# Feature-major products with the tokens' high and low halves side by side in one 512-column matmul

## The chip, the core and the metric

The kernel runs on one core of a Trainium2 chip. The metric is the device time of one execution in microseconds (us); lower is better. TensorE is called PE here, VectorE DVE, ScalarE ACT, GpSimd POOL, and SyncE (which issues the weight transfers) SP. PEld is TensorE's loading of the stationary operand.

## The reference

The program computes two transformer blocks on 256 tokens of width 1024, in float32. The first block (latent attention beside a gated convolution, then a 32-expert mixture) is not touched by the change. The second block is, cut to what matters:

```python
u = rms_norm_2(h, norm_mix)
proj = u @ w_in                       # z_pool 512, q 512, k 128, v 128, g_pool 1024, g_attn 1024
y_pool = multiscale_pool(z_pool, w_pool_group, pool_scale) @ w_pool_branch
y_attn = windowed_gqa(q, k, v, sink) @ w_attn_branch
merged = sigmoid(g_pool) * y_pool + sigmoid(g_attn) * y_attn
h = h + merged @ w_out
u = rms_norm_2(h, norm_ffn)
h = h + (silu(u @ w_ffn_gate) * (u @ w_ffn_up)) @ w_ffn_down   # hidden width 2816
return rms_norm_2(h, norm_final)
```

## The kernel before

A matrix product is made of three products of rounded halves: a float32 value is split into a high half (a rounded copy, made by ACT) and a low half (the rest, a subtraction on DVE), and `high*high + high*low + low*high` is accumulated in one PSUM tile. `mm3` (L275) issues these three matmuls for each piece of 128 contracted rows.

The weights come as one stream of pieces of 128x1024 values (two to one DMA of 1 MB, tile `raw`, seven buffers). `Stream.split` casts a piece to its high half `whi` on ACT (L116) and subtracts to get the low half `wlo` on DVE (L119), each in a ring of five buffers; `W.ahead` keeps up to four pieces split ahead of the one in use, and `W.take` hands out the next. A cast of a new piece waits until PE has finished with the piece five before it, whose buffer it takes.

In block 2 a product is either "rows" (tokens stationary, 512 columns of weights moving) or "feature-major" (weights stationary, the 256 tokens moving, output 128 features x 256 tokens). The feature-major ones are made by `features` (L287): eight pieces k, each with three matmuls of 256 columns: weights' high half with the tokens' high half (L279), weights' high half again with the tokens' low half (L280), weights' low half with the tokens' high half (L281). The transposed tokens are in `uTh` and `uTl` (attention and pooling) and `u2h` and `u2l` (feed-forward), each 128 x 8 x 256. One piece of weights (128x1024) is just what one feature-major product uses.

The feature-major products through `u_block` and `ff_first` are, in order: four of the pooling input (`zp`, `pool_in`, L1362), eight gates of the pooling branch (`gt` into `gp`, L1396), eight gates of the attention branch (`gt` into `ga`), and in the feed-forward part, for each of 20 hidden blocks f, a gate and an up product (`gu`, `ff_first`, L1553). In between stand the small products of the attention: scores (`s2a`, `s2b`), transposed probabilities (`pT`), values (`av`), and the pooling groups' products (`pg`, L1387), and later the branch products (`br`) and the output product (`o`). The result in PSUM is multiplied on DVE by `R`, the tokens' norm factors spread over all partitions (L1367, L1399, L1559), and then pooled, or sent through Tanh or Silu on ACT.

In the feed-forward loop (L1597) each f issues the down product (`f`, "rows") of block f-2 (nine matmuls of 512 columns and six of 256), then gate and up of f; after the loop stand the down products of blocks 18 to 21. `hidden` splits the activated block into `sh` (ACT) and `sl` (DVE).

PSUM tiles come from two pools of four (`mmt`, `acct`). A scheduler puts each engine's instructions in order from the order in which the code issues them, its own costs, and the data they need; the queues then run strictly in that order.

Of the kernel before, what the change touches and what calls it, by code (L numbers as in the profile page):

```python
# [11 lines left out]
F32 = mybir.dt.float32  # L12
F32R = mybir.dt.float32r
BF16 = mybir.dt.bfloat16
I32 = mybir.dt.int32
AF = mybir.ActivationFunctionType
ALU = mybir.AluOpType
# [3 lines left out]
P = 128  # L21
D = 1024
NM = 16
S = 256
# [34 lines left out]
def block_kernel(ctx, tc, rwt, x, meta, pos, wst, gains, cst, pvec, rbias, sink, wpg, cst2, out):  # L59
    nc = tc.nc  # L60
    PE, ACT, DVE, POOL = nc.tensor, nc.scalar, nc.vector, nc.gpsimd
# [5 lines left out]
    def mmt(name):  # L67
        return ps.tile([P, 512], F32, name=name, tag="mm", bufs=4)
# [110 lines left out]
    W = Stream()  # L179
# [20 lines left out]
    def sm(w, p=P):  # L200
        return keep.tile([P, w], F32, name=f"sm{w}", tag=f"sm{w}", bufs=12)[:p]
# [49 lines left out]
    def stt(o, a, sc, b, op0=ALU.mult, op1=ALU.mult):  # L251
        return DVE.scalar_tensor_tensor(o, a, sc, b, op0=op0, op1=op1)  # L252
# [15 lines left out]
    small, pace, last_mm = [], [1], [None]  # L268

    def fill(n=None):  # L270

        for _ in range(len(small) if n is None else min(n, len(small))):
            small.pop(0)()

    def mm3(o, pairs, first=True, last=True):  # L275

        n = len(pairs)
        for i, (sh, sl, mh, ml) in enumerate(pairs):
            PE.matmul(o, sh, mh, start=first and i == 0, stop=False, skip_group_check=True)  # L279
            PE.matmul(o, sh, ml, start=False, stop=False, skip_group_check=True)  # L280
            last_mm[0] = PE.matmul(o, sl, mh, start=False, stop=last and i == n - 1, skip_group_check=True)  # L281
            fill(pace[0])

    def kb(w, k, n=P):
        return w[:, k * n:(k + 1) * n]

    def features(o, w, ah, al, c0, n):  # L287

        mm3(o, [(kb(w[0], k), kb(w[1], k), ah[:, k, c0:c0 + n], al[:, k, c0:c0 + n])
                for k in range(8)])  # L290

    def rows(o, w, ah, al, n, first, last):

        mm3(o, [(ah, al, kb(w[0], n, 512), kb(w[1], n, 512))], first=first, last=last)
# [82 lines left out]
    with tc.tile_pool(name="p1", bufs=1) as p1:  # L377
# [3 lines left out]
        start = ExitStack()  # L381
# [69 lines left out]
        def in_block(name, c0, n, psum=mmt):  # L451
            o = psum(name)[:, :n]
            features(o, W.take(), hth, htl, c0, n)
            return o
# [21 lines left out]
        o, w = mmt("cq")[:, :S], W.take()  # L476
        for z, (wz, az) in enumerate(((0, hth), (0, htl), (1, hth))):
            for k in range(8):
                PE.matmul(o, kb(w[wz], k), az[:, k, NM:], start=z + k == 0, stop=z == 2 and k == 7,
                          skip_group_check=True)  # L480
# [55 lines left out]
        R = p1.tile([P, T], F32, name="R")  # L536
# [118 lines left out]
        w = W.take()  # L655
        for j in range(4):
            o = mmt("kn")[:, :T]
# [208 lines left out]
    with tc.tile_pool(name="p2", bufs=1) as p2:  # L866
# [3 lines left out]
        th = p2.tile([P, 2, D], F32R, name="tkh")  # L870
        tl = p2.tile([P, 2, D], F32R, name="tkl")
# [11 lines left out]
        o = mmt("lg")  # L883
        for i in range(2):
            for k in range(8):
                PE.matmul(o[:, i * 36:(i + 1) * 36], tT[:, k, i * P:(i + 1) * P], kb(rw, k, 36), start=k == 0,
                          stop=k == 7, skip_group_check=True)
# [55 lines left out]
        for c in (0, S):  # L943
            for i in range(2):
                oh_ins = DVE.tensor_scalar(oh[:, i, c:c + S], cs[:, C_IOTA + c:C_IOTA + c + S], code[:, i:i + 1],
                                           None, op0=ALU.is_equal)
        PE.matmul(rk[:, 8:16], ones, gz[:, 1:].rearrange("p a b -> p (a b)"), start=True, stop=True,
                  skip_group_check=True)
# [158 lines left out]
        for ex in range(N_EXP):  # L1107
            g, e = divmod(ex, 8)
            xg = xgs[g][:, :D], xgs[g][:, D:]
            gu = mmt("gu")  # L1110
# [56 lines left out]
        with tc.If(many > 0):  # L1167
# [11 lines left out]
            for g in range(4):  # L1179
# [3 lines left out]
                for b in range(2):  # L1183
                    for a in range(4):
                        for i in range(2):
                            for src in (th, tl):
                                PE.matmul(kb(pa, a), kb(src[:, i], 4 * b + a).bitcast(F32), ohx[:, i],
                                          start=i == 0 and src is th, stop=i == 1 and src is tl,
                                          skip_group_check=True)
# [44 lines left out]


    with tc.tile_pool(name="p3", bufs=1) as p3:
        uTh = p3.tile([P, 8, S], F32R, name="uTh", tag="th")
        uTl = p3.tile([P, 8, S], F32R, name="uTl", tag="tl")
        with tc.tile_pool(name="p3a", bufs=1) as q3:
            c2 = q3.tile([P, 64 + 512], F32, name="c2")  # L1240
            POOL.dma_start(c2, cst2)
# [8 lines left out]
            R = q3.tile([P, S], F32, name="R2")  # L1250
# [3 lines left out]
            def pw(name):  # L1254
                return q3.tile([P, PW], F32, name=name, tag="pw", bufs=5)

            def u_block(name):
                o = mmt(name)[:, :S]
                features(o, W.take(), uTh, uTl, 0, S)
                return o  # L1260


# [99 lines left out]
            def pool_in(g):  # L1362
                zp = pw("zp")
                POOL.memset(zp[:, :8], 0.0)
                POOL.memset(zp[:, 8 + S:], 0.0)
                o = u_block("zp")
                DVE.tensor_mul(zp[:, 8:8 + S], o, R)  # L1367
                W.ahead()
                s, lo, hi = zp, 0, PW
                for m in range(g + 1):  # L1370
                    d = pw("ws")
                    a, b = (1, 0) if m == 0 else (2 ** (m - 1), 2 ** (m - 1))
                    lo, hi = lo + a, hi - b
                    DVE.tensor_add(d[:, lo:hi], s[:, lo - a:hi - a], s[:, lo + b:hi + b])
                    s = d
                w = 2.0 ** (g + 1)
                res = pw("res")[:, :S]
                stt(res, s[:, 8:8 + S], 1.0 / w, zp[:, 8:8 + S], ALU.mult, ALU.subtract)
                for c0 in (0, S - 8):
                    e = c2[:, g * 16:g * 16 + 8] if c0 == 0 else c2[:, g * 16 + 8:g * 16 + 16]  # L1380
                    DVE.tensor_mul(res[:, c0:c0 + 8], s[:, 8 + c0:16 + c0], e)
                    DVE.tensor_sub(res[:, c0:c0 + 8], res[:, c0:c0 + 8], zp[:, 8 + c0:16 + c0])
                return res
# [12 lines left out]
            def gates(dst, js):  # L1396
                for j in js:
                    o = u_block("gt")
                    DVE.tensor_mul(dst[:, j], o, R)  # L1399
                    ACT.activation(dst[:, j], dst[:, j], AF.Tanh, scale=0.5)  # L1400
                    W.ahead()

# [36 lines left out]
            def branch(gt, sh, sl, js, done=None):  # L1439
                for j in js:  # L1440
# [8 lines left out]
                    if done:  # L1449
                        done(j)  # L1450

            res = [pool_in(0)]
            scores2(0, 0)
            scores2(0, 2)
            es0 = softmax2(0)
            pool_group(0, res[0])
            res.append(pool_in(1))
            scores2(1, 0)
            scores2(1, 2)
            es1 = softmax2(1)  # L1460
            pool_group(1, res[1])
            res.append(pool_in(2))
            denom(0, es0)
            pTx = [q3.tile([P, 2, 512], F32, name="pTa", **kw) for kw in ({}, {"tag": "q4"})]
# [4 lines left out]
            pool_group(2, res[2])  # L1469
            values2(0, 0)  # L1470
            gates(gp, (0, 1))
            pool_group(3, res[3])
            values2(0, 1)
            denom(1, es1)
            probs_T2(1, 0)
            at0 = attn_out(0)
            gates(gp, (2, 3))
            probs_T2(1, 1)
            values2(1, 0)
            gates(gp, (4,))  # L1480
            values2(1, 1)
            at1 = attn_out(1)
# [27 lines left out]
            nx = [normed(0, o2[0], g_f2, s2)]  # L1510
            with tc.issue_after(merged[0].ins):
                ACT.activation(sm(1), ones[:, :1], AF.Silu)
            u2h = p3.tile([P, 8, S], F32R, name="u2h", tag="th")
            u2l = p3.tile([P, 8, S], F32R, name="u2l", tag="tl")

            def first_T(k):
                if k == 5:
# [4 lines left out]
        with tc.tile_pool(name="p3b", bufs=1) as q3:  # L1522
            R = q3.tile([P, S], F32, name="R3")
            hids = {}

            def hidden(f, src, c0=0, n=S):
                if f not in hids:
                    hids[f] = (q3.tile([P, S], F32R, name="sh", tag="sh", bufs=6),
                               q3.tile([P, S], F32R, name="sl", tag="sl", bufs=6))
                split(src, *[t[:, c0:c0 + n] for t in hids[f]])  # L1530
# [20 lines left out]
                    hidden(f, kb(ht, f), i * P, P)  # L1551

            def ff_first(f):  # L1553
                o = mmt("gu2")
                for b in range(2):
                    features(o[:, b * S:(b + 1) * S], W.take(), u2h, u2l, 0, S)
                    W.ahead()
                gu = q3.tile([P, 2, S], F32, name="gu", tag="gu", bufs=2)
                DVE.tensor_tensor(gu, o.rearrange("p (a t) -> p a t", a=2),  # L1559
                                  R[:, None, :].to_broadcast([P, 2, S]), op=ALU.mult)  # L1560
                ACT.activation(gu[:, 0], gu[:, 0], AF.Silu)
                DVE.tensor_mul(gu[:, 0], gu[:, 0], gu[:, 1])
                hidden(f, gu[:, 0])

# [28 lines left out]
            f2[1] = [f2[1][0], f2[1][1][:, :S], mmt("f212")[:, :S]]  # L1593
            rows_act(0, o_r[0])
            ff_first(2)
            rows_act(1, o_r[1])
            for f in range(3, 22):  # L1597
                for d in ([0, 1] if f == 3 else [f - 2] if f < 20 else []):
                    w = W.take()
                    for i in range(2):  # L1600
                        down(d, w, i)
                    W.ahead()
                ff_first(f)
# [198 lines left out]
```

## Time and profile before

| | us |
|---|---|
| median of 3 runs (798.35 to 801.41) | 799.4 |
| the profiled execution | 799.25 |
| its span | 797.5 |
| PE busy | 768.4 (96%) |
| PEld busy | 669.7 (84%) |
| DVE busy | 613.8 (77%) |
| ACT busy | 470.4 (59%) |

The span runs from the first to the last profiled instruction; 1.75 us of the execution lie around it. The times of matmuls overlap, so the busy time of PE is no measure of how densely it works; the distance between the starts of two neighbouring matmuls is. Times in the rows below are counted from the start of the span. Block 2's feature-major products begin at 476.8 us and end at 779.0 us.

### The profile page before, as it was taken

What the parts mean: (1) busy time and instruction counts of PE and PEld (TensorE: products, weight loads), DVE (VectorE), ACT (ScalarE), POOL (GpSimd) and SP (SyncE); (2) the same over time, 40 slices, a digit from 0 to 9 for tenths busy, and PEclk for the clock granted to TensorE, in tenths of its full rate; (3) what the DMA queues carried; (4) which work ended last, traced back from release to release, by engine and by line L of the source; (5) the groups of instructions that cost most, each with busy time, mean ns of one, the idle gap of its engine ahead of it and who ended that gap; (6) DMA issues with size and microseconds to landing.
All of it is one profiled execution on the core that took longest, in us unless ns stands there. A gap on an engine that the chain in (4) does not pass through costs nothing. (4 is left out here: it accounts for less than half of the span.)

```text
span 797.5 us, 11994 instructions
## 1 busy us (share of the span) xinstructions
PE 768.4 (96%) x4587; PEld 669.7 (84%) x4587; DVE 613.8 (77%) x983; ACT 470.4 (59%) x699; POOL 65.1 (8%) x70
## 2 busy tenths in 40 slices
PE   7989999999999999999999879999999999999996
PEld 5979985788888888888777668999988999999995
DVE  5878678899999989998986769856768566566565
ACT  4646445588788888887777345534556444444442
POOL 5631200000000000000003330000000000000000
PEclk9989999999999999999999999999999999999998
DMA  8736354699889979998998432445445455545101
GB/s 335 302 106 246 112 205 158 229 369 369 310 316 365 366 294 368 373 367 311 361 367 308 163 122 106 144 138 195 159 159 212 164 205 166 204 167 204 54 1 53
DMA packets 27217, 182.53 MB, mean 229 GB/s; under 512 B 3328, under 2 KB 3584, under 8 KB 6160
## 3 DMA queue, kind: packets, MB, share of 16 engines
q1 hardware_dynamic: 25344, 176.96, 59.8%
q0 software_dynamic: 1056, 3.71, 1.4%
q10 hardware_dynamic: 752, 1.01, 0.4%
q8 instruction: 38, 0.62, 0.3%
q14 instruction: 27, 0.22, 0.1%
HBM read 180.62 MB, written 1.05 MB: 228 GB/s over the span
## 5 line engine op out<-in xcount | busy, mean ns | idle before, releaser
L116 ACT CAST whi<-raw 128x1024 fp32r<-128x1024 f32 x328 | 339.8, 1049 | 186.6 <-PE gu L280 49.1
L119 DVE TENSOR_TENSOR wlo<-raw,whi 128x1024 fp32r<-128x1024 f32 x318 | 384.4, 1226 | 83.8 <-ACT whi L116 76.8
L279 PE MATMUL gu<-whi,xg 128*128 128x512 f32 x256 | 102.8, 401 | 0.0
L280 PE MATMUL gu<-wlo,xg 128*128 128x512 f32 x256 | 101.3, 396 | 0.0
L281 PE MATMUL gu<-whi,xg 128*128 128x512 f32 x256 | 100.7, 393 | 0.0
L280 PE MATMUL gu<-u2l,whi 128*128 128x256 f32 x320 | 90.6, 283 | 0.0
L279 PE MATMUL gu<-u2h,whi 128*128 128x256 f32 x320 | 90.6, 283 | 0.0
L281 PE MATMUL gu<-u2h,wlo 128*128 128x256 f32 x320 | 90.6, 283 | 0.0
L280 PEld LDWEIGHTS gu<-u2l,whi 128*128 128x128 f32 x320 | 61.5, 192 | 0.0
L281 PEld LDWEIGHTS gu<-u2h,wlo 128*128 128x128 f32 x320 | 61.4, 192 | 0.0
L279 PEld LDWEIGHTS gu<-u2h,whi 128*128 128x128 f32 x320 | 61.4, 192 | 0.0
L280 PEld LDWEIGHTS gu<-wlo,xg 128*128 128x128 f32 x256 | 48.2, 188 | 11.2 <-DVE wlo L119 1.4
L281 PEld LDWEIGHTS gu<-whi,xg 128*128 128x128 f32 x256 | 48.0, 188 | 10.5
L279 PEld LDWEIGHTS gu<-whi,xg 128*128 128x128 f32 x256 | 48.1, 188 | 9.9
L281 PE MATMUL y<-whi,hl 128*128 128x512 f32 x128 | 50.5, 394 | 0.0
L280 PE MATMUL y<-wlo,hh 128*128 128x512 f32 x128 | 50.5, 394 | 0.0
L119 POOL TENSOR_TENSOR wlo<-raw,whi 128x1024 fp32r<-128x1024 f32 x10 | 24.3, 2443 | 309.8 <-ACT whi L116 309.3
L279 PE MATMUL y<-whi,hh 128*128 128x512 f32 x128 | 48.7, 397 | 0.0
L279 PE MATMUL f<-whi,sh 128*128 128x512 f32 (+1 forms) x110 | 38.2, 349 | 0.0
L280 PE MATMUL f<-wlo,sh 128*128 128x512 f32 (+1 forms) x110 | 38.1, 349 | 0.0
L281 PE MATMUL f<-whi,sl 128*128 128x512 f32 (+1 forms) x110 | 37.8, 348 | 0.0
L279 PE MATMUL gt<-uTh,whi 128*128 128x256 f32 x128 | 36.7, 287 | 0.0
(468 smaller groups left out, 1529.8 us busy)
## 6 DMA issues: line engine op xcount, KB each, us to landing
raw<-in_wst_dram SPq DMA_DIRECT2D x164, 1024.0 KB, 4.8
gain<-in_gains_dram POOLq DMA_DIRECT2D x6, 512.0 KB, 4.3
raw<-in_wst_dram SPq DMA_DIRECT2D x5, 512.0 KB, 8.5
h<-in_x_dram SPq DMA_DIRECT2D x2, 512.0 KB, 4.8
cs<-in_cst_dram SPq DMA_DIRECT2D x1, 612.0 KB, 17.1
out_dram<-mg SPq DMA_DIRECT2D x2, 256.0 KB, 2.6
out_dram<-mg ACTq DMA_DIRECT2D x2, 256.0 KB, 2.8
c<-in_cst_dram POOLq DMA_DIRECT2D x1, 288.0 KB, 3.0
```

Of the source, the lines that this page charges most:

```text
L116: ACT.copy(hi, src)
L119: eng.tensor_sub(lo, src, hi.bitcast(F32))
L279: PE.matmul(o, sh, mh, start=first and i == 0, stop=False, skip_group_check=True)
L280: PE.matmul(o, sh, ml, start=False, stop=False, skip_group_check=True)
L281: last_mm[0] = PE.matmul(o, sl, mh, start=False, stop=last and i == n - 1, skip_group_check=True)
```

## The change

The tokens' halves are stored side by side (`uT`, `u2`: 128 x 8 x 2 x 256), so that for each k high and low half are 512 neighbouring columns. A new function `both` takes the place of `features` in block 2: for each k one matmul of 512 columns with the weights' high half as the stationary operand (its left 256 columns of output gather high*high, its right 256 high*low), and one of 256 columns with the weights' low half, added to the left part. A product now fills a PSUM tile of 512 columns, and its two parts are added when it is read: `scaled` copies the right part to SBUF on ACT, adds the left part on DVE, and multiplies by `R` on DVE. In `ff_first`, gate and up have had one tile of 512 columns for both and one multiplication of 512 columns; now each has its own tile and its own three steps.

```diff
+    def both(o, w, a):
+        for k in range(8):
+            PE.matmul(o, kb(w[0], k), a[:, k].rearrange("p z t -> p (z t)"), start=k == 0, stop=False,
+                      skip_group_check=True)
+            last_mm[0] = PE.matmul(o[:, :S], kb(w[1], k), a[:, k, 0], start=False, stop=k == 7, skip_group_check=True)
+            fill(pace[0])
+
+    def scaled(dst, o, R):
+        ACT.copy(dst, o[:, S:])
+        DVE.tensor_add(dst, dst, o[:, :S])
+        DVE.tensor_mul(dst, dst, R)
...
-        uTh = p3.tile([P, 8, S], F32R, name="uTh", tag="th")
-        uTl = p3.tile([P, 8, S], F32R, name="uTl", tag="tl")
+        uT = p3.tile([P, 8, 2, S], F32R, name="uT", tag="thl")
+        uTh, uTl = uT[:, :, 0], uT[:, :, 1]
...
             def u_block(name):
-                o = mmt(name)[:, :S]
-                features(o, W.take(), uTh, uTl, 0, S)
+                o = mmt(name)
+                both(o, W.take(), uT)
                 return o
...
-                DVE.tensor_mul(zp[:, 8:8 + S], o, R)
+                scaled(zp[:, 8:8 + S], o, R)
...
-                    DVE.tensor_mul(dst[:, j], o, R)
+                    scaled(dst[:, j], o, R)
                     ACT.activation(dst[:, j], dst[:, j], AF.Tanh, scale=0.5)
...
             def ff_first(f):
-                o = mmt("gu2")
+                gu = q3.tile([P, 2, S], F32, name="gu", tag="gu", bufs=2)
                 for b in range(2):
-                    features(o[:, b * S:(b + 1) * S], W.take(), u2h, u2l, 0, S)
+                    o = mmt("gu2")
+                    both(o, W.take(), u2)
                     W.ahead()
-                gu = q3.tile([P, 2, S], F32, name="gu", tag="gu", bufs=2)
-                DVE.tensor_tensor(gu, o.rearrange("p (a t) -> p a t", a=2),
-                                  R[:, None, :].to_broadcast([P, 2, S]), op=ALU.mult)
-                ACT.activation(gu[:, 0], gu[:, 0], AF.Silu)
+                    scaled(gu[:, b], o, R)
+                    if b == 0:
+                        ACT.activation(gu[:, 0], gu[:, 0], AF.Silu)
                 DVE.tensor_mul(gu[:, 0], gu[:, 0], gu[:, 1])
                 hidden(f, gu[:, 0])
```

Lines behind L290 move down by 15 in the changed kernel. How instructions stand is shown at three places. First PE, in a feed-forward up product, before:

```order
L279 MATMUL gu_8276<-u2h,whi 128x256
L280 MATMUL gu_8276<-u2l,whi 128x256
L281 MATMUL gu_8276<-u2h,wlo 128x256
L279 MATMUL gu_8276<-u2h,whi 128x256
L280 MATMUL gu_8276<-u2l,whi 128x256
L281 MATMUL gu_8276<-u2h,wlo 128x256
```

and the same place now (`u` is the tile `u2` with both halves):

```order
L296 MATMUL gu_7990<-u_6325,whi 128x512
L298 MATMUL gu_7990<-u_6325,wlo 128x256
L296 MATMUL gu_7990<-u_6325,whi 128x512
L298 MATMUL gu_7990<-u_6325,wlo 128x256
```

Three matmuls of 256 columns have become one of 512 and one of 256, so the columns are the same 768 and one matmul and one load of the stationary operand are gone for each k.

Second DVE, where the first pooling product is read, before (`wlo_5170` and `wlo_5255` are the low halves of the first and second gate product's weights, `zp_5143` the PSUM tile, `zp_5140` the SBUF tile):

```order
L119 TENSOR_TENSOR wlo_5170<-raw_4249,whi_5169 128x1024
L1367 TENSOR_TENSOR zp_5140<-zp_5143,R2_4865 128x256
L1374 TENSOR_TENSOR ws_5173<-zp_5140 128x271
L119 TENSOR_TENSOR wlo_5255<-raw_4249,whi_5254 128x1024
L252 SCALAR_TENSOR_TENSOR res_5175<-ws_5173,zp_5140 128x256
L252 SCALAR_TENSOR_TENSOR pr0_5128<-c2_4856,s2a_5181 128x256
```

and now:

```order
L119 TENSOR_TENSOR wlo_5163<-raw_4249,whi_5162 128x1024
L119 TENSOR_TENSOR wlo_5242<-raw_4249,whi_5241 128x1024
L304 TENSOR_TENSOR zp_5139<-zp_5139,zp_5142 128x256
L252 SCALAR_TENSOR_TENSOR pr0_5127<-c2_4855,s2a_5174 128x256
L305 TENSOR_TENSOR zp_5139<-zp_5139,R2_4864 128x256
L252 SCALAR_TENSOR_TENSOR pr0_5127<-c2_4855,s2a_5174 128x256
L1389 TENSOR_TENSOR ws_5166<-zp_5139 128x271
```

The multiplication has become an addition and a multiplication, and the second subtraction of weights has moved ahead of both.

Third ACT, in the feed-forward loop, two blocks f before:

```order
L1561 ACTIVATE gu<-gu 128x256
L74 CAST sh<-gu 128x256
L116 CAST whi<-raw 128x1024 x3
L1561 ACTIVATE gu<-gu 128x256
L74 CAST sh<-gu 128x256
L116 CAST whi<-raw 128x1024 x3
```

and one block f now (`gu_6707` and `gu_6734` are the PSUM tiles of gate and up):

```order
L303 COPY gu<-gu_6707 128x256
L116 CAST whi<-raw 128x1024
L1576 ACTIVATE gu<-gu 128x256
L303 COPY gu<-gu_6734 128x256
L116 CAST whi<-raw 128x1024
L74 CAST sh<-gu 128x256
L116 CAST whi<-raw 128x1024
```

Two copies out of PSUM have come in, each ahead of a cast of weights.

## Rows read from the trace of the kernel before

**Rows 1.** The page's engine list: busy us, share of the span, instructions.

```profile
PE 768.4 (96%) x4587; PEld 669.7 (84%) x4587; DVE 613.8 (77%) x983; ACT 470.4 (59%) x699; POOL 65.1 (8%) x70
```

**Rows 2.** Waits of PE, 470 to 797 us: total us, times, longest.

```profile
PE pg L1387 <- DVE res L1382: 1.8, 2, 1.3
```

**Rows 3.** Stretches: length, busy us of PE, PEld, DVE, ACT, POOL; PEclk, DMA, GB/s.

```profile
477.00:498.00 21.00, 19.21 (x152) 17.36 (x151) 20.04 (x54) 12.40 (x28) 0.28 (x4) 1.00 0.28 101
498.00:531.00 33.00, 33.00 (x280) 32.84 (x280) 23.42 (x51) 16.21 (x38) 0.14 (x2) 1.00 0.36 128
531.00:566.00 35.00, 35.00 (x295) 35.00 (x294) 22.08 (x30) 15.77 (x22) 0.00 (x0) 1.00 0.53 181
...
619.00:779.00 160.00, 160.00 (x1187) 152.93 (x1187) 96.72 (x115) 71.07 (x96) 0.00 (x0) 1.00 0.41 145
```

**Rows 4.** Instruction groups on PE by shape: count, busy us, mean ns, idle.

```profile
L279 PE MATMUL gu<-u2h,whi 128*128 128x256 f32 x320 | 90.6, 283 | 0.0
...
L279 PE MATMUL gt<-uTh,whi 128*128 128x256 f32 x128 | 36.7, 287 | 0.0
...
L279 PE MATMUL f<-whi,sh 128*128 128x512 f32 x66 | 25.9, 395 | 0.0
...
L279 PE MATMUL zp<-uTh,whi 128*128 128x256 f32 x32 | 9.2, 289 | 0.0
```

**Rows 5.** Timeline of PE: start us, us; 48 matmuls between these two.

```profile
633.59 0.28 PE L279 MATMUL gu<-u2h,whi 128*128 128x256 f32 x1
...
639.35 0.40 PE L279 MATMUL f<-whi,sh 128*128 128x512 f32 x1
```

**Rows 6.** Timeline of PE, a down product: nine of 512 columns.

```profile
630.81 0.40 PE L279 MATMUL f<-whi,sh 128*128 128x512 f32 x1
...
632.65 0.39 PE L281 MATMUL f<-whi,sl 128*128 128x512 f32 x1
...
632.87 0.28 PE L279 MATMUL f<-whi,sh 128*128 128x256 f32 x1
```

**Rows 7.** Timeline of PE, the output product: 78 of 512 columns between these.

```profile
577.50 0.39 PE L279 MATMUL o<-whi,mgh 128*128 128x512 f32 x1
...
595.68 1.04 PE L259 MATMUL tr<-ident,mg 128*128 128x128 f32 x8
```

**Rows 8.** Timeline of DVE and PE in the pooling stage.

```profile
480.20 0.42 DVE L1367 TENSOR_TENSOR zp<-zp,R 128x256 f32<-128x256 f32 x1 [0.81 <-PE zp L281]
...
481.22 1.23 DVE L119 TENSOR_TENSOR wlo<-raw,whi 128x1024 fp32r<-128x1024 f32 x1
...
496.95 1.22 DVE L119 TENSOR_TENSOR wlo<-raw,whi 128x1024 fp32r<-128x1024 f32 x1
...
507.48 0.36 PE L279 MATMUL gt<-uTh,whi 128*128 128x256 f32 x1
```

**Rows 9.** Instruction groups on ACT and DVE by shape, 440 to 797 us.

```profile
L74 ACT CAST yph<-yp 128x256 fp32r<-128x256 f32 x4 | 1.6, 404 | 0.2 <-DVE yp L1389 0.2
...
L1559 DVE TENSOR_TENSOR gu<-gu,R 128x512 f32<-128x512 f32 x20 | 13.8, 692 | 12.8 <-PE gu L281 12.8
...
L1399 DVE TENSOR_TENSOR gp<-gt,R 128x256 f32<-128x256 f32 x8 | 3.4, 420 | 6.0 <-PE gt L281 6.0
```

**Rows 10.** Timeline of the feed-forward part: a cast, and the last block's chain.

```profile
648.01 1.05 ACT L116 CAST whi<-raw 128x1024 fp32r<-128x1024 f32 x1 [1.82 <-PE gu L280]
...
659.21 0.28 PE L279 MATMUL gu<-u2h,whi 128*128 128x256 f32 x1
...
779.17 0.69 DVE L1559 TENSOR_TENSOR gu<-gu,R 128x512 f32<-128x512 f32 x1 [0.55 <-PE gu L281]
...
781.30 0.42 DVE L75 TENSOR_TENSOR sl<-gu,sh 128x256 fp32r<-128x256 f32 x1 [0.47 <-ACT sh L74]
...
783.07 0.39 PE L279 MATMUL f<-whi,sh 128*128 128x512 f32 x1
```

More of the change, by code (lines that the diff above doesn't have):

```diff
@@ L1512, in block_kernel @@
                 ACT.activation(sm(1), ones[:, :1], AF.Silu)
-            u2h = p3.tile([P, 8, S], F32R, name="u2h", tag="th")
-            u2l = p3.tile([P, 8, S], F32R, name="u2l", tag="tl")
+            u2 = p3.tile([P, 8, 2, S], F32R, name="u2", tag="thl")
+            u2h, u2l = u2[:, :, 0], u2[:, :, 1]
             def first_T(k):
```

## The prediction, made before the changed kernel had run

> **What bounds the kernel now.** The page comes first: PE is busy 96% of the span [rows 1]. A busy share alone doesn't say that an engine is the limit, so I read the waits of PE from 470 us on, where block 2's products stand: there is a single row, 1.8 us for the pooling groups' products behind DVE [rows 2]. Then the stretches: from 498 to 566 and from 619 to 779 us PE is busy every microsecond at a granted clock of 1.00, the upper level of 2.4 GHz, while DVE has idle time (96.72 of 160 us in the feed-forward part) and ACT more [rows 3]. Only from 477 to 498 us is DVE the fuller engine, 20.04 of 21 us, and PE lacks 1.79 us. So nearly all that the change touches is bound by how densely PE issues matmuls, and the pooling stage is the place to watch.
>
> How densely, the timeline shows. A feed-forward pair of gate and up has 48 matmuls of 256 columns in 639.35 - 633.59 = 5.76 us, 120.0 ns from start to start [rows 5]. The means in the groups, 283 ns for 256 columns and 395 ns for 512 [rows 4], are lengths of overlapping instructions and price nothing here. For 512 columns a down product has nine in 632.87 - 630.81 = 2.06 us, 228.9 ns each [rows 6], and the output product 78 in 18.18 us, 233.1 ns [rows 7]. 256 columns at 2.4 GHz are 106.7 ns, so a matmul of 256 costs 13.3 ns beyond its columns, and one of 512 costs 15.6 to 19.8 ns beyond its 213.3. That small cost per matmul is all that this change can save on PE, since 768 columns stay 768.
>
> **The change part by part.** Removed: one matmul (with its load of the stationary operand) for each k. There are 320 + 128 + 32 = 480 such k [rows 4], the counts of L279 in gu, gt and zp. Before, a k costs 3 x 120.0 = 360.0 ns. After, it is one of 512 and one of 256. The trace of before has no alternation of the two, so I bound it: 228.9 + 120.0 = 348.9 ns by the down product, which runs in the same stage with the same neighbours; 233.1 + 120.0 = 353.1 ns by the output product; and, lowest, the step from a 512 to a 256, where 632.65 to 632.87 is 0.22 us [rows 6], which gives 220 + 120 = 340 ns if each 256 after a 512 starts so early. I take 348.9, from the nearest row. The saving is 11.1 ns x 480 = 5.3 us; the bounds are 3.3 us and 9.6 us.
>
> The Trainium skill (TensorE: Matmul & The Clock Gate, "Back-to-back issue gap") gives a warm matmul N/2.4 + 2.5 ns, 109.2 for 256 columns and 215.8 for 512. By that rule a k saves only 2.5 ns, an estimate of 1.2 us in all, and the change would be worth nothing that can be measured; the 120.0 ns of [rows 5] is above its 109.2, so I don't sum with it, but it is one of the rivals.
>
> Added on ACT: 60 copies of 128x256 out of PSUM. The nearest row of that shape takes 404 ns [rows 9], so 60 x 0.40 = 24 us, beside PE: ACT has 160 - 71.07 = 89 us idle in the feed-forward part, where 40 of them fall. Added on DVE: in each of the 20 pooling and gate products one multiplication of 0.42 us [rows 9] becomes an addition and a multiplication, +0.42; in each of the 20 feed-forward blocks one multiplication of 0.69 us becomes four instructions of 0.42, +0.99. That is 8.4 + 19.8 = 28 us of DVE, 20 of them in a stage with 63 us of idle time. I cost both at nothing there.
>
> What keeps the cover is the distance at which weights are split. A copy on ACT now waits for the end of a product, and behind it in the queue stands a cast of weights. But that cast had to wait for the same thing: the one at 648.01 was released by the end of a gu product, and the piece that it makes is first used at 659.21, 11.2 us later [rows 10]. Cast and subtraction take 1.05 + 1.23 us, one copy and two DVE steps in front of them 1.24 us more; about 7.7 us are left. If that cover went, each of the 40 products could lose the 1.24 us, 50 us in all, and only then would the sum be lost. The subtraction's end also frees the buffer for the next transfer on SP; the order of SP is the same as before, and the transfers use 0.41 of the queues' time.
>
> The chain at the end: the last block's gate and up are read at 779.17, and its low half is ready at 781.30 + 0.42 = 781.72, while the down product that uses it starts at 783.07 [rows 10], 1.35 us later. Before, it begins with a multiplication of 0.69 us and Silu, an ACT instruction of 256 columns like the cast's 0.40 [rows 9]: 1.09. Now the gate is done one product earlier, and the up part begins with a copy of 0.40, an addition and a multiplication of 0.42: 1.24. What follows is the same on both sides, so 0.15 us of the 1.35 are used up, and it stays covered.
>
> The pooling stage: DVE is full from 480 us on [rows 3], and gets an addition for each of the four pooling products and, as its fullness ends somewhere in the next stretch, about four gates: 8 x 0.42 = 3.4 us. The order also sets the subtraction for the second gate product ahead of the first addition. Its cast takes the buffer of the first pooling product's weights and so begins only when that product has ended; DVE did the multiplication and the first pooling sum in that time, from 480.20 to 481.22 [rows 8], and now stands still there, about 0.8 us. Against 4.2 us of delay stand these margins: the low half for the third gate product is finished at 496.95 + 1.22 = 498.17 and first used at 507.48 [rows 8], 9.3 us later. So weights are not late. The pooling groups' products may be: two of the four gave the 1.8 us of waits, and DVE reaches them later. But PE has other products to issue meanwhile, and it gains 96 x 11.1 ns = 1.1 us in this stage before it has to wait. I put what is added to the waits and what is won elsewhere in the stage at nothing, with bounds of -1 and +2 us.
>
> Sum: the profiled execution took 799.25 us (span 797.5 and 1.75 around it), the median of the runs is 799.4, 0.15 higher. 799.25 - 5.3 = 793.95 us; I say 794.0.
>
> **The rivals.**
> 1. A tighter pair. If the 256 behind a 512 always starts after 220 ns, a k costs 340 ns, the saving is 9.6 us and the time 789.7. For it speaks the one step in [rows 6]; against it that a single step is read in hundredths of a microsecond and the nine before it take 228.9 on average.
> 2. No gain worth measuring: a matmul of 512 costs more beyond its columns than one of 256. With the output product's 233.1 the saving is 3.3 us and the time 795.9. Further out, a 512 might cost as much as two of 256, 240 ns, and nothing is saved: 799.3. By the Trainium skill's issue gap (same page and section as above) the saving would be the 1.2 us estimated there, near that outer end. For it speaks that 512 already costs 2 to 6 ns more beyond its columns; against it, that no row of 512 columns in block 2's steady stretches reaches 240.
> 3. Slower: the pooling stage takes over. DVE is full there, copy on ACT, addition and multiplication now follow each other for each of the stage's 12 products (four zp, eight gates), and if PE, in strict order, waits for all of it at the pooling groups, the scores' tiles and the probabilities, the stage grows by 12 x 0.42 + 0.8 = 5.8 us if DVE's additions count alone, or 12 x 0.82 + 0.8 = 10.6 us with the copies. The other 48 products still win 384 x 11.1 ns = 4.3 us. That gives 800.8 to 805.6. It decides from the point on where PE's waits between 477 and 531 us grow by more than the 4.3 us. For it speaks DVE's 20.04 of 21 us; against it the 9.3 us of margin for the weights and that the stage's backlog ends before the gates do.
> 4. The change saves a load of 192 ns or the difference of the groups' means, 3 x 283 - (395 + 283) = 171 ns a k, 82 us in all: 717. The start-to-start distances of [rows 5] speak against it; I give it 1 in 100.
>
> **How the numbers follow.** Forecast 0.50, rival 1 0.14, rival 2 0.25, rival 3 0.10, rival 4 0.01. A difference of 0.5%, 4.0 us, is about what a measurement of this kernel can tell from no change; faster means below 795.4, slower above 803.4. The forecast's own range is 792 to 795.4. Faster: 0.50 + 0.14 + 0.01 = 0.65. Rival 2 lies within 0.5%, and of rival 3 about 0.03, so same 0.28; slower 0.07. The range reaches from rival 1's 789.7 to the outer half of rival 2, 798.5, and leaves out the rest of rivals 2, 3 and 4, under 0.2.
>
> **What would show each step right or wrong.** In the changed profile a feed-forward pair of gate and up should take 16 x 0.349 = 5.58 us from start to start, where it takes 5.76; 5.44 would be rival 1, 5.65 and more rival 2. The last gu product should end about 5 us earlier than before, and the waits of PE behind 470 us should stay below 4 us. If the pairs take 5.58 us and the time is still above 797, the pooling stage or the end has eaten it. If PE shows waits for `whi` or `wlo` in the feed-forward loop, I was wrong about the distance of the splits.

## The result, and the profile after

The changed kernel takes 796.25 us (median of 15 runs, 793.3 to 798.57), the kernel before, run beside it, 800.71 (15 runs, 798.09 to 804.02). The ratio is 0.9945 with a 95% interval of 0.9931 to 0.996, so 4.4 us are gone, 3.2 to 5.5 by the interval. Forecast were 794.0 us, from 5.3 us of saving; the whole range of 789.5 to 798.5 holds the measured time, the forecast's own 792 to 795.4 does not. The profiled execution took 795.85 us, 3.4 less than the profiled one before.

The page's engine list of the changed kernel answers to [rows 1]:

```profile
PE 765.4 (96%) x4107; PEld 644.1 (81%) x4107; DVE 635.9 (80%) x1063; ACT 486.5 (61%) x759; POOL 65.0 (8%) x70
```

and PE's waits from 470 to 797 us (total, times, longest) to [rows 2]:

```profile
PE pg L1402 <- DVE res L1397: 1.1, 1, 1.1
```

480 matmuls and 480 loads are gone, and 80 instructions came to DVE and 60 to ACT. PE waits no more than before: 1.1 us, where it was 1.8. What was added on the other engines is not waited for.

Two profiled executions already differ in front of block 2's products, so I cut the span at starts of matmuls that both kernels have. The timeline of PE (start, length), before:

```profile
476.84 0.28 PE L279 MATMUL zp<-uTh,whi 128*128 128x256 f32 x1
...
530.56 0.28 PE L279 MATMUL br<-yph,whi 128*128 128x256 f32 x1
...
542.08 0.28 PE L279 MATMUL gt<-uTh,whi 128*128 128x256 f32 x1
...
565.97 0.28 PE L279 MATMUL br<-ath,whi 128*128 128x256 f32 x1
...
612.55 0.61 PE L374 MATMUL rs<-dg,ones 128*128 128x128 f32 x4
...
778.97 0.40 PE L279 MATMUL f<-whi,sh 128*128 128x512 f32 x1
```

and after, with two feed-forward pairs of gate and up in between:

```profile
477.85 0.40 PE L296 MATMUL zp<-uT,whi 128*128 128x512 f32 x1
...
530.71 0.28 PE L279 MATMUL br<-yph,whi 128*128 128x256 f32 x1
...
542.23 0.39 PE L296 MATMUL gt<-uT,whi 128*128 128x512 f32 x1
...
565.68 0.28 PE L279 MATMUL br<-ath,whi 128*128 128x256 f32 x1
...
612.24 0.61 PE L389 MATMUL rs<-dg,ones 128*128 128x128 f32 x4
...
641.20 0.40 PE L296 MATMUL gu<-u,whi 128*128 128x512 f32 x1
...
646.85 0.40 PE L279 MATMUL f<-whi,sh 128*128 128x512 f32 x1
...
649.65 0.40 PE L296 MATMUL gu<-u,whi 128*128 128x512 f32 x1
...
655.21 0.40 PE L279 MATMUL f<-whi,sh 128*128 128x512 f32 x1
...
775.57 0.40 PE L279 MATMUL f<-whi,sh 128*128 128x512 f32 x1
```

Subtracting neighbours gives the stretches (us; `rs` is the matmul that spreads the norm factors for the feed-forward part):

| stretch | before | after | difference |
|---|---|---|---|
| pooling stage, first `zp` to first `br` (96 changed k) | 53.72 | 52.86 | -0.86 |
| branch and one stretch of gates, `br` to second `br` (64 k) | 35.41 | 34.97 | -0.44 |
| second branch and output product, to `rs` | 46.58 | 46.56 | -0.02 |
| feed-forward, `rs` to the first `f` behind the last `gu` (320 k) | 166.42 | 163.33 | -3.09 |
| sum | | | -4.41 |

The first `zp` starts 1.01 us later in this profile; that start varies between profiles whatever the edit (last section). The 4.41 us behind it and the ratio's 4.4 us agree. Behind the last row of the table both have 18.53 us.

What keeps those stretches is seen in their windows (length; busy us of PE, PEld, DVE, ACT, POOL; granted clock; DMA share; GB/s). Before:

```profile
476.84:530.56 53.72, 51.93 (x427) 49.92 (x426) 43.37 (x103) 28.29 (x64) 0.42 (x6) 1.00 0.33 118
612.55:778.97 166.42, 166.42 (x1240) 159.25 (x1239) 101.41 (x122) 73.97 (x101) 0.00 (x0) 1.00 0.42 151
```

and after, with the two pairs and the down products behind them:

```profile
477.85:530.71 52.86, 51.78 (x332) 44.78 (x330) 46.12 (x113) 30.87 (x74) 0.42 (x6) 1.00 0.34 120
612.24:775.57 163.33, 163.33 (x920) 141.63 (x918) 117.11 (x180) 84.26 (x140) 0.00 (x0) 1.00 0.43 154
641.20:649.65 8.45, 8.45 (x49) 7.30 (x48) 6.01 (x11) 4.31 (x7) 0.00 (x0) 1.00 0.60 201
649.65:657.97 8.32, 8.32 (x50) 7.26 (x48) 5.91 (x10) 4.30 (x7) 0.00 (x0) 1.00 0.47 174
```

PE is busy in every microsecond of the feed-forward part in both kernels, at a granted clock of 1.00, the upper level; DVE rises by 15.7 us and ACT by 10.3 and both keep idle time. The pairs take 5.65 and 5.56 us in turn, where a pair of before took 5.76 [rows 5].

### The profile page after: what moved, and what is told of

Its sections match the earlier page's. It is cut to its first block, busy times and chain, and to the rows that moved or that the text cites. A ratio compares the mean times of both kernels' runs of the same rounds, so it can differ in the third digit from the quotient of the medians.

```text
span 794.1 us, 11174 instructions
## 1 busy us (share of the span) xinstructions
PE 765.4 (96%) x4107; PEld 644.1 (81%) x4107; DVE 635.9 (80%) x1063; ACT 486.5 (61%) x759; POOL 65.0 (8%) x70
## 3 DMA queue, kind: packets, MB, share of 16 engines
q10 hardware_dynamic: 752, 1.01, 0.4%
## 5 line engine op out<-in xcount | busy, mean ns | idle before, releaser
L296 PE MATMUL gu<-u,whi 128*128 128x512 f32 x320 | 113.1, 397 | 0.0
L298 PE MATMUL gu<-u,wlo 128*128 128x256 f32 x320 | 89.5, 280 | 0.0
L296 PEld LDWEIGHTS gu<-u,whi 128*128 128x128 f32 x320 | 60.1, 188 | 13.7
L298 PEld LDWEIGHTS gu<-u,wlo 128*128 128x128 f32 x320 | 60.4, 189 | 0.0
L281 PEld LDWEIGHTS gu<-whi,xg 128*128 128x128 f32 x256 | 48.0, 188 | 10.5
L296 PE MATMUL gt<-uT,whi 128*128 128x512 f32 x128 | 45.6, 399 | 0.0
L298 PE MATMUL gt<-uT,wlo 128*128 128x256 f32 x128 | 36.2, 283 | 0.0
L281 PEld LDWEIGHTS y<-whi,hl 128*128 128x128 f32 x128 | 24.1, 188 | 5.6
```

Of the source, the lines that this page charges most:

```text
L296: PE.matmul(o, kb(w[0], k), a[:, k].rearrange("p z t -> p (z t)"), start=k == 0, stop=False, skip_group_check=True)
L298: last_mm[0] = PE.matmul(o[:, :S], kb(w[1], k), a[:, k, 0], start=False, stop=k == 7, skip_group_check=True)
```

## The experiments

My theory: the saving is one matmul's fixed cost beyond its columns for each k, and the reading on ACT and DVE is hidden. Rivals: the gain comes from something else than the merge (the order of the casts, two PSUM tiles); the reading costs part of it; or what is saved is a load, because loads and not columns set PE's pace. The measured kernel is the changed one with the edit shown. "Before" ran beside each on the same chip. The scheduler made a new order for every edited kernel: in the pooling stage PE's order differs from the changed kernel's a little in experiment 1, and more in 2, 4, 5 and the first part of 3.

**1. Three matmuls again, everything else as changed.**

```diff
-            PE.matmul(o, kb(w[0], k), a[:, k].rearrange("p z t -> p (z t)"), start=k == 0, stop=False,
+            PE.matmul(o[:, :S], kb(w[0], k), a[:, k, 0], start=k == 0, stop=False, ...)
+            PE.matmul(o[:, S:], kb(w[0], k), a[:, k, 1], start=k == 0, stop=k == 7, ...)
```

> Undoes the merge alone: each k again has three matmuls of 256 columns, but high*low goes to the right half of the tile, and the reading (copy on ACT, addition and multiplication on DVE) stays as in the changed kernel. Theory A (PE saves a fixed cost per matmul, the reading is hidden): a feed-forward pair of gate and up takes 5.76 us again (changed: 5.60 on the mean), from the spread's first matmul to the last gu product's end 166.4 us as before (changed: 163.3), ratio to the kernel before 0.998 to 1.003. Theory B (the gain is that consecutive matmuls no longer all add to the same columns): the pair takes less than 5.70 us here too and the ratio is below 0.997. Theory C (the reading is not hidden and eats part of the gain): PE shows waits over 4 us behind 470 us and the ratio is above 1.003.

Measured: 799.77 us (12 runs), before 801.34; ratio 0.9975 (0.9958 to 0.9992). By my reading the left half's first high*high term isn't in the sum here; the number of instructions and their sizes are those of the whole sum. The timeline of PE in this kernel:

```profile
613.05 0.61 PE L389 MATMUL rs<-dg,ones 128*128 128x128 f32 x4
...
634.00 0.28 PE L296 MATMUL gu<-u,whi 128*128 128x256 f32 x1
...
639.76 0.40 PE L279 MATMUL f<-whi,sh 128*128 128x512 f32 x1
...
779.38 0.40 PE L279 MATMUL f<-whi,sh 128*128 128x512 f32 x1
```

and its waits from 470 us on:

```profile
PE pg L1402 <- DVE res L1397: 1.2, 1, 1.2
```

The pair is back at 5.76 us and the feed-forward part at 166.33; the pooling stage takes 53.67 where before took 53.72. With the whole reading in place nothing behind 450 us is longer or shorter than before, so the gain that the stretches show is the merge's alone; theory B is out, since the right half gets its own columns here too and the pair gains nothing. The times say less: 0.9975 is a little under the 0.998 that I expected, and against the changed kernel's 0.9945 it puts only 0.3 of the 0.55% on the merge. The rest is not found in any stretch; experiment 7 gives how far such a ratio can be trusted.

**2. Less reading: high*low is left out of what is read** (one multiplication, no copy and no addition).

```diff
-        ACT.copy(dst, o[:, S:])
-        DVE.tensor_add(dst, dst, o[:, :S])
-        DVE.tensor_mul(dst, dst, R)
+        DVE.tensor_mul(dst, o[:, :S], R)
```

> Leaves out the added reading: the merged matmuls stay, but the result is read by one multiplication of the left half (high*low is computed and dropped from the result). Theory A (reading hidden): pair 5.60 us, ratio within 0.1% of the changed kernel's 0.9945, PE's waits behind 470 us 1 to 2 us. Theory C (reading costs): faster than the changed kernel by more than 1 us, and the time from the first pooling product to the first branch product falls clearly below the changed kernel's 52.9 us (before: 53.7), to 51.5 or less. If the excess of the 512-column matmul over 226.7 ns comes from ACT and DVE reading and writing beside it, the pair falls to 5.55 us.

Measured: 797.38 us (7 runs); ratio 0.994 (0.9918 to 0.9961), where the changed kernel has 0.9945. The timeline of PE:

```profile
615.52 0.61 PE L387 MATMUL rs<-dg,ones 128*128 128x128 f32 x4
...
778.90 0.40 PE L279 MATMUL f<-whi,sh 128*128 128x512 f32 x1
```

163.38 us in the feed-forward part against 163.33 with the reading; the pooling stage takes 52.66 against 52.86. Without 60 copies and 60 additions (20 multiplications of 256 columns more than before remain) nothing more than 0.2 us is won in a stretch, about as much as the changed kernel's own stretches differ between two profiles (experiment 7): the reading is hidden, and it isn't what makes a 512-column matmul cost more than its columns either.

**3. The change in one part only.** First in the feed-forward part alone (`zp` and gates again by `features` and one multiplication), then in the pooling and gate products alone:

```diff
             def u_block(name):
-                o = mmt(name)
-                both(o, W.take(), uT)
+                o = mmt(name)[:, :S]
+                features(o, W.take(), uTh, uTl, 0, S)
...
-                    scaled(dst[:, j], o, R)
+                    DVE.tensor_mul(dst[:, j], o, R)
```

> The change in the feed-forward part alone; the 20 pooling and gate products as before. Theory A: 320 of the 480 k, 320 x 9.7 ns = 3.1 us, ratio 0.996; pair 5.60 us; from the first pooling product to the first branch product 53.7 us as before. If the pooling stage loses by the change, this is as fast as the whole change or faster.

```diff
             def ff_first(f):
+                o = mmt("gu2")
...
-                    both(o, W.take(), u2)
+                    features(o[:, b * S:(b + 1) * S], W.take(), u2h, u2l, 0, S)
```

> The change in the 20 pooling and gate products alone; feed-forward as before. Theory A: 160 of the 480 k, 160 x 9.7 ns = 1.6 us, ratio 0.998; pair 5.76 us; first pooling product to first branch product 52.9 us, the eight gates behind the first branch products from 23.9 to 23.5 us. Theory D (the pooling stage takes over): slower than before, waits of PE over 4 us in that stage.

Measured: feed-forward alone 797.71 us (10 runs), ratio 0.9959 (0.994 to 0.9978); its feed-forward part takes 163.11, its pooling stage 53.71. Pooling and gates alone 800.28 (12 runs), ratio 0.9977 (0.9962 to 0.9991); pooling stage 52.86, second gates 23.44 (before 23.89), feed-forward 166.41. 0.41% and 0.23% add up to 0.64%, within the intervals of the whole's 0.55%; so do the stretches, 4.6 us here and 4.41 there. Nothing shows that the two parts act on each other. The second ratio is no lower than experiment 1's, so for the 1.3 us of pooling and gates the stretches are the evidence, not the times.

**4. A shorter low matmul**: high*low of the weights only for the first 128 tokens, 128 columns in place of 256.

```diff
-            last_mm[0] = PE.matmul(o[:, :S], kb(w[1], k), a[:, k, 0], start=False, ...)
+            last_mm[0] = PE.matmul(o[:, :P], kb(w[1], k), a[:, k, 0, :P], start=False, ...)
```

> The low-half matmul takes only the first 128 tokens (low*high of the others is left out), so each k is one matmul of 512 columns and one of 128. If a matmul's distance is its columns at 2.4 GHz and a fixed cost (theory A, 13.3 ns), the k falls by 53 ns, from 350 to 297 ns, and a gate-and-up pair from 5.60 to 4.75 us. If the distance is set by the loading of the stationary operand (theory E: what the change saves is a load, and a load can't be had more often than every 120 ns or so), the short matmul takes about as long as the one of 256 columns, the k stays at 340 to 350 ns, the pair at 5.4 to 5.6 us.

Measured: 811.37 us in one run (before 801.43), slower. Two things are to be read. The first is the pair, here the timeline of PE and of its loads:

```profile
642.91 0.40 PE L296 MATMUL gu<-u,whi 128*128 128x512 f32 x1
643.15 0.22 PE L298 MATMUL gu<-u,wlo 128*128 128x128 f32 x1
643.15 0.19 PEld L296 LDWEIGHTS gu<-u,whi 128*128 128x128 f32 x1
643.21 0.45 PE L296 MATMUL gu<-u,whi 128*128 128x512 f32 x1
643.26 0.19 PEld L298 LDWEIGHTS gu<-u,wlo 128*128 128x128 f32 x1
643.50 0.23 PE L298 MATMUL gu<-u,wlo 128*128 128x128 f32 x1
...
648.32 0.44 PE L279 MATMUL f<-whi,sh 128*128 128x512 f32 x1
```

128 columns fewer are 53 ns fewer at 2.4 GHz, and theory A's pair was 4.75 us; the pair took 5.41 us, 338 ns for a k, only 12 less than the changed kernel's 350. So theory A missed here, and the number is theory E's. The 512 starts 0.06 us behind the 128, but the next 128 comes 0.29 later, and two loads never start less than 0.11 us apart. A 128-column matmul with its own load thus takes up about 338 - 229 = 109 ns (229 by the down product [rows 6]), not the 67 of columns and fixed cost. The Trainium skill (TensorE: Matmul & The Clock Gate, "LDWEIGHTS (loading the stationary operand)") gives a load columns/1.2 ns, 106.7 for these 128: the 0.11 us from start to start agree, the recorded length of 0.19 does not.

Is the 120.0 ns of 256 columns such a floor too? The timeline of PE in the kernel before has two groups that tell, each at a granted clock of 1.00: 21 matmuls of 272 columns from the first to the second line, and 16 of 64 columns from the third to the fourth:

```profile
58.43 0.29 PE L279 MATMUL xin<-hth,whi 128*128 128x272 f32 x1
...
61.08 0.29 PE L281 MATMUL gc<-hth,wlo 128*128 128x272 f32 x1
...
503.28 1.89 PE L1428 MATMUL av<-vt,pTa 128*128 128x64 f32 x16
...
504.98 0.36 PE L279 MATMUL gt<-uTh,whi 128*128 128x256 f32 x1
```

64 columns take 106 ns each, within 3 ns of the 128 columns here, so with loads of this recorded length there is a floor, 106 to 109 ns. 272 columns take 126, 6 more than 256, and 16 columns at 2.4 GHz are 6.7: from 256 on the columns set the distance, and theory E's load every 120 ns doesn't hold. The floor is under the 120.0, so saving a load as such gives nothing there; at 64 or 128 columns it would. What the 13.3 ns beyond the columns are isn't shown.

The second is why the kernel got slower with less work on PE. Windows of its pooling stage and its second branch:

```profile
500.00:510.00 10.00, 8.61 (x57) 7.55 (x55) 10.00 (x26) 8.73 (x26) 0.14 (x2) 1.00 0.16 44
510.00:520.00 10.00, 9.55 (x41) 9.14 (x42) 6.36 (x23) 2.90 (x6) 0.00 (x0) 0.54 0.43 168
583.00:590.00 7.00, 5.26 (x31) 5.05 (x31) 5.81 (x13) 4.58 (x9) 0.00 (x0) 0.76 0.50 172
```

and PE's waits from 470 to 815 us:

```profile
PE pg L1402 <- DVE res L1397: 4.8, 3, 1.9
...
PE br L279 <- DVE ga L304: 2.7, 2, 1.7
```

PE ran out of products ahead of a full DVE (10.00 of 10.00 us) and waited three times for the pooling groups, and behind that the granted clock was 0.54 on the mean of 10 us, near the lower level of 1.2 GHz. The pooling stage took 63.32 us, 10.5 more than in the changed kernel, and the second branch 16.33 where it took 11.51; the feed-forward part still won 1.95. That is what my rival 3 foretold, brought about by a shorter PE, or by its order: the third pair of `pg` products stands behind 26 gate matmuls here, behind 49 in the changed kernel. The two were not separated.

**5. More on DVE in the pooling stage**: an idle maximum of a tile with itself behind each of the 12 products, once, and four times.

```diff
+            def more(t):
+                for _ in range(1):      # 4 in the second kernel
+                    DVE.tensor_tensor(t, t, t, op=ALU.max)
...
                 scaled(zp[:, 8:8 + S], o, R)
+                more(zp[:, 8:8 + S])
...
                     scaled(dst[:, j], o, R)
+                    if dst is gp:
+                        more(dst[:, j])
```

> The changed kernel with one more DVE instruction (maximum of the block with itself, 128x256, about 0.42 us) behind each of the pooling stage's 12 products: 5.0 us more on DVE, which has 6.7 us idle between the first pooling and the first branch product. Theory A (the stage has cover left): that stretch stays at 52.9 us, within 0.6. Theory D (DVE is the limit there already): it grows by 4 to 5 us.

> The same with four such instructions for each of the 12 products, 20 us, more than DVE's 6.7 us of idle time. Both theories expect PE to wait now; if the two engines' times simply have to fit, the stretch grows by 20 - 6.7 = 13 us, to 66; if part of the stage's DVE work can move behind the first branch product, by less, 5 to 10 us. PE's waits grow from 1.1 us by as much.

Measured, one run each beside a kernel before of 801.43: 797.5 and 806.09 us. With one more, 12 x 0.42 = 5.0 us of DVE, the pooling stage takes 53.55, 0.69 more than in the changed kernel, a little past the 0.6 that I gave it; nothing behind it moves. With four, 20 us, it takes 56.58, 3.7 more and not the 5 to 13 that I expected, and the branch behind it 16.89 instead of 11.52, 9.1 us in all. Windows of the kernel with four:

```profile
540.00:545.00 5.00, 2.10 (x15) 1.71 (x14) 5.00 (x14) 1.36 (x2) 0.00 (x0) 1.00 0.38 162
545.00:552.14 7.14, 7.14 (x49) 7.14 (x49) 6.30 (x11) 1.47 (x2) 0.00 (x0) 0.76 0.79 294
```

and PE's waits from 470 to 815 us in it:

```profile
PE br L279 <- DVE gp L252: 2.1, 1, 2.1
...
PE gt L298 <- DVE wlo L119: 1.4, 1, 1.4
```

PE waits there for what DVE makes, late weights among it, 6.9 us with three further rows, and the branch's clock is below 1.00 behind it. So the cover is real and has an edge: 5 us more are nearly free, 20 us cost half of themselves. That is with the scheduler's new order: with four, the first `pg` products stand behind 51 of the 64 pooling matmuls, behind 31 in the changed kernel. The change, by which DVE's busy time in the stage rose from 43.37 to 46.12 us (windows in the first section), is on the free side.

**6. The change in the 16 branch products too.** Their high and low halves are put side by side (`yp2`, `atv2`), `both` gets the number of k, and the sum is read by a copy, an addition and the gating.

```diff
-                    o = mmt("br")[:, :S]
-                    mm3(o, [(kb(w[0], c0 + k), kb(w[1], c0 + k), sh[:, k], sl[:, k]) for k in range(4)])
+                    o = mmt("br")
+                    both(o, [x[:, (j % 2) * 512:(j % 2) * 512 + 512] for x in w], a, 4)
...
-                    stt(gt[:, j], gt[:, j], 1.0, o, ALU.add, ALU.mult)
+                    bt = pw("bt")[:, :S]
+                    ACT.copy(bt, o[:, S:])
+                    DVE.tensor_add(bt, bt, o[:, :S])
+                    stt(gt[:, j], gt[:, j], 1.0, bt, ALU.add, ALU.mult)
```

> The changed kernel with the same merge in the 16 branch products too (64 more k: high and low halves of the pooled and attended tokens side by side; read by a copy on ACT, an addition on DVE and the gating). Theory A: 64 x 9.7 ns = 0.6 us, each stretch of eight branch products from 11.52 to 11.2 us, ratio to the kernel before 0.994 where the changed one has 0.9945; all other stretches as in the changed kernel. If the longer chain behind the last branch product of the attention is not hidden, the output product behind it starts with a wait and the gain is gone.

> The branch products merged too, again: 0.6 us below the changed kernel by its stretches (11.20 us for eight branch products where the changed kernel has 11.52); the ratio 0.992 to 0.995, which these rounds may not tell from the changed kernel's.

Measured: 795.35 us (6 runs), ratio 0.9927 (0.9901 to 0.9953); again 796.88 (10 runs), 0.9944 (0.9923 to 0.9965). Timeline of PE, the first branch stretch in the first profile:

```profile
531.51 0.40 PE L296 MATMUL br<-yp,whi 128*128 128x512 f32 x1
...
542.71 0.40 PE L296 MATMUL gt<-uT,whi 128*128 128x512 f32 x1
```

The branch stretches take 11.20 and 11.22 us, 0.3 less each (11.24 and 11.21 in the second profile): 64 k at 9.5 ns, the same saving again. 0.6 us is below what the runs tell apart, so this version is the changed kernel's equal by its times and better only by its stretches.

**7. The kernel before and the changed kernel once more**, nothing edited.

> The kernel before against itself, to see how far a ratio of this kernel can be trusted, since the three-matmul kernel came out at 0.9975 although each stretch of its trace from 450 us on is as before within 0.1 us. If the comparison is sound to its interval, the ratio is 0.9985 to 1.0015 and the 0.9975 has a cause of its own in front of 450 us. If the time in front of 450 us (the waits behind the conditional branch, 3.8 to 6.3 us in the profiles so far) moves between loads of a program, ratios of 0.997 to 1.003 come from nothing.

> The changed kernel again, on the same chip as the next one: ratio 0.993 to 0.996; from the spread's first matmul to the end of the last gu product 163.3 us, first pooling to first branch product 52.9 us.

Measured: the kernel before against itself 0.9993 (0.9976 to 1.0009), with medians of 799.51 and 800.57, 1.1 us apart for one program. The changed kernel again: 796.59 us (11 runs), 0.9948 (0.9928 to 0.9969), with 53.03 us in its pooling stage (52.86 in the first profile) and 163.11 in its feed-forward part (163.33). The result stands. By what I wrote beforehand, a ratio this near 1 gives experiment 1's 0.9975 a cause of its own in front of 450 us; but the two intervals overlap, and whether anything is behind it stays open.

## Why the prediction was right, and which term was mis-sized

- **The saving for each k.** Forecast 360.0 - 348.9 = 11.1 ns. Measured 3.09 us / 320 = 9.7 ns in the feed-forward part, 0.86 / 96 = 9.0 in the pooling stage, 0.44 / 64 = 6.9 in the second gates. The sum came to 4.4 us instead of 5.3. The mis-sized term is the 348.9 ns of a changed k, for which I took a 512 from the down product's 228.9 ns [rows 6]: the pairs come in two lengths, 5.56 us (16 k at 347.5 ns) and 5.65 (353.1, just the bound by the output product [rows 7]), and 353.1 would give the 6.9 of the second gates as well. I had a row for either and chose the one; the mean of both bounds, 351 ns, would have given 4.3 us. Only the k is sure: by the starts in the changed kernel's two profiles, the step behind a 512 is 232 to 237 ns (means over the shorter and the longer pairs) and the step behind a 256 is 114 to 117, so neither the 228.9 nor the 120.0 came true by itself, and the two errors partly cancel.
- **The time.** 796.25 is 2.3 us above my 794.0: 0.9 is the saving, and 1.3 is the kernel before, which took 800.71 here and not 799.4. It lies above the 795.4 that I had set for faster; the ratio, 0.55%, is just beyond the 0.5% that this stood for. So the 0.65 for faster is not clearly borne out.
- **Rival 1**, 340 ns, is not seen; the one early step in [rows 6] didn't repeat. **Rival 2** came nearest among the rivals, and nearly as near as the forecast: half of the pairs have its k of 353.1 ns, and 4.4 us lie between its 3.3 and the forecast's 5.3. By the Trainium skill's "Back-to-back issue gap" (TensorE: Matmul & The Clock Gate) an estimated 1.2 us were to be won; 4.4 are measured, and the measurement decides. **Rival 4**, 82 us, is out by the 4.4 us themselves.
- **The reading costs nothing.** Right: the copies took 362 ns (404 by forecast) and the additions 414, as these groups of the changed kernel (440 to 797 us) show, and PE doesn't wait in the feed-forward loop; experiments 1 and 2 show it from both sides.

```profile
L303 ACT COPY gu<-gu 128x256 f32<-128x256 f32 x40 | 14.5, 362 | 1.3 <-PE gu L298 1.3
...
L304 DVE TENSOR_TENSOR gu<-gu,gu 128x256 f32<-128x256 f32 x40 | 16.6, 414 | 0.0
```

- **The chain at the end.** Right: 0.15 us of the margin used up. The timeline of the changed kernel, to be held against [rows 10]:

```profile
778.05 0.42 DVE L75 TENSOR_TENSOR sl<-gu,sh 128x256 fp32r<-128x256 f32 x1 [0.47 <-ACT sh L74]
...
779.67 0.39 PE L279 MATMUL f<-whi,sh 128*128 128x512 f32 x1
```

The low half is ready at 778.47, and the down product that uses it starts 1.20 us later, where it was 1.35.

- **The pooling stage.** Forecast: nothing, with -1 and +2 as bounds; it took 0.86 us less, about its 96 k's whole saving; the 0.7 us less of waits isn't it, since experiment 1, with 1.2 us of waits and nothing merged, takes as long as before. The hole that the order foretold is there, and larger, 1.67 us instead of 0.8 (DVE, changed kernel):

```profile
482.07 1.23 DVE L119 TENSOR_TENSOR wlo<-raw,whi 128x1024 fp32r<-128x1024 f32 x1 [1.67 <-ACT whi L116]
```

It and the additions (3.4 us by forecast, 2.75 more of DVE's busy time in the stage's windows) were absorbed: PE's waits did not grow. **Rival 3** asked for waits that grow by more than 4.3 us; they fell by 0.7. Experiment 5 puts its point of decision between 5 and 20 us of further DVE work.

## What to carry to other kernels

Price a merge of matmuls by the distance from start to start in steady stretches, never by the mean lengths in the groups: here the latter gave 82 us, the former 5.3, and 4.4 came. Where every matmul has 256 columns or more, as here, a matmul saved is worth only some 10 ns (at 64 and 128 columns a floor of 106 to 109 ns for matmul and load would count); look for rows of the merged size in several places, and where they differ, sum by the mean. Added reading on engines beside PE was free here, where what they make stands several microseconds ahead of its use in the feed-forward loop, and 1.20 us at the end; that margin can be read beforehand and should be tested by doubling the added work.

## What the runs showed of the hardware that I had not expected

- The same matmuls in one and the same loop come at two distances, in turn from pair to pair: 347.5 and 353.1 ns for a k of 512 and 256 columns. The down products behind the pairs alternate with them, 2.80 and 2.76 us (first section), while before all pairs took 5.76. It isn't the reading (experiment 2 has both), nor the load on the transfers: in the changed kernel the longer cycle has the higher DMA share (0.60 against 0.47, windows in the first section), in the kernel of experiment 3 with the feed-forward part alone it is the other way round:

```profile
632.52:640.98 8.46, 8.46 (x49) 7.30 (x48) 5.95 (x9) 4.30 (x7) 0.00 (x0) 1.00 0.47 173
640.98:649.30 8.32, 8.32 (x50) 7.26 (x48) 5.96 (x10) 4.30 (x7) 0.00 (x0) 1.00 0.61 204
```

  What makes the two levels stays open.
- Less work on PE went with a kernel 10 us slower in its one run (experiment 4), and the granted clock was below 1.00 (0.54 and 0.76) in the stretches behind PE's waits; it was also 0.76 behind 5 us in which PE was busy for 2.10 (experiment 5). Which share of the loss is the waits and which the clock wasn't separated.
- The first product of block 2's attention begins between 449.1 and 453.6 us in the thirteen profiles, although all edits stand behind it; two profiles of experiment 6's kernel are 1.0 us apart. 4.5 us is as much as the change is worth, so a single profile's span can't judge it, and stretches between matmuls can.
